# Two pieces of deferred work in a chunked scan: sums of squares in the next scan's first step, the sample's state in its second

## The chip, the core and the metric

The kernel runs on one core of a Trainium2 chip. The metric is device time in microseconds (us) of one execution, as the median of several runs. The core has engines that each run their own instructions in order and meet through semaphores: TensorE (PE in the profile, PEld for its weight loads), VectorE (DVE), ScalarE (ACT), GpSimd (POOL) and SyncE (SP), which issues most DMAs.

## What is computed

A trunk of two layers for 1024 prompt tokens and 64 sample tokens (8 sequences of 8), 1024 channels wide, in float32. The first layer is a Mamba-2 mixer, the second a pooling mixer. The change lies in the first layer, in the scan over the sequence and the gated norm behind it. Cut to that:

```python
def ssd_branch(h, conv_prev, ssm_prev, ...):
    zxbcdt = h @ w_in                                  # z, x, B, C, dt
    xbc_act = silu(conv(xbc))
    ...
    y, new_ssm = ssd_scan(xs, dt, A, Bm, Cm, ssm_prev) # 32 heads in 8 groups, chunks of 128 tokens
    y = y + d_skip * xs
    gated = (y * silu(z)).reshape(b, L, 8, 256)        # 8 groups of 256 channels
    gated = gated * rsqrt(mean(gated * gated, -1) + EPS)
    return (gated * norm_g) @ w_out, new_conv, new_ssm

def ssd_scan(x, dt, A, B, C, h0):
    ...
    chunk_states = einsum('bctgn,bctgr,bctgrp->bcgrpn', B, decay_end, xdt)
    h = chunk_decay * h + chunk_states                 # from chunk to chunk
    y_inter = einsum('bctgn,bctgr,bcgrpn->bctgrp', C, exp(acum), h_prev)
    return y_intra + y_inter, h_final
```

The sample's sequences have one chunk of 8 tokens each, start from a given state h0, and give back a new state (`new_ssm`), which is an output.

## The kernel before

Channels lie on the 128 partitions, tokens along the free dimension (1024 prompt tokens and 64 sample tokens, 1088 columns). After a first stage the eight channel groups g = 0 to 7 are scanned one after the other (`ssd_layer`, `scan`). A scan has four steps p = 0 to 3, each for two chunks of 128 prompt tokens. A step has transposes and products of the next chunks (`scan_front`, PSUM tiles `tr`), the chunk states (`scan_state`, PSUM tile `S`, states `h`), the decay matrices of the next step (`scan_decay`: a DMA broadcasts the cumulated log decays into the single buffer `acb`, ACT makes `ea`, `M` and `cd` from it, DVE multiplies) and the output (`scan_y`, PSUM tiles `y`, added into `xs` by L587). Step 2 also holds the front of the 64 sample tokens (`sample_front`, `sample_inter` with tile `Z`), step 3 their output (`sample_y`).

Between these, TensorE works off units of a fill stream (`fills`): the input projection of the next groups, three units of 24 matmuls for each tile of 128 channels (PSUM tiles `mm`, evicted by ACT in L433 and L435, then convolved). The last tile, (7, 3), is done in eight units over all three `mm` buffers at once. After it the stream goes over to the output projection: rows of gated outputs come back from DRAM (`row<-gyd`, L1583), ACT and DVE split them into two parts (`b<-row`, L1088 and L1089), and products `op<-b,w` follow. `PACE` says how many units each step takes.

TensorE's order is the order in which the code is written; on the other engines and in SP's DMA queue a scheduler orders the instructions, by when it thinks that they can run. Tiles of one row of tokens come from a ring of slots (`Slots`): a slot goes to the tile that asks next, and who had it before decides what that tile waits for.

Four pieces of a scan's end are deferred into the next scan:

- `gate_rows(s)`, at the end of step 3: DVE multiplies the outputs by the gate (L710), ACT squares them (L711).
- `gate_norm(last)`: 16 matmuls with ones sum the squares over channels (PSUM tile `ms`, of the two `y` buffers), ACT takes Ln and Exp (L722, L723), a DMA writes the result out (`rsd`) and another reads it back to all partitions (`rs<-rsd`).
- `gate_scale(last)`: DVE multiplies by it (L732, twice), two DMAs store the rows (`gyd<-xbc`, L734).
- `sample_state(last)`: 16 matmuls give the sample's new state (PSUM tiles `S`: both `y` buffers, the `S` buffer and one `mm` buffer), DVE adds it (L696, four times), two DMAs store it (`hsT`, L697). `sample_load(s)` behind it loads the next sample state (`h<-h0T`) and `acs`.

Of the kernel before, what the change touches and what calls it, by code (L numbers as in the profile page):

```python
# [106 lines left out]
class Build:  # L107
# [1411 lines left out]
    def scan(self, s, fill):  # L1519

        g = s.g
        last, after = self.scans[g - 1] if g else None, self.scans[g + 1] if g < 7 else None
        for p in range(4):
            a, b, c = PACE[g][p]
            self.units(fill, a)
            if p < 3:
                self.scan_front(s, p + 1)
            self.scan_state(s, p)
            if p < 3:
                self.scan_decay(s, p + 1)  # L1530
                if p < 2:
                    self.scan_ac(s, p + 2)
                elif after:
                    self.scan_ac(after, 0)
            self.units(fill, b)
            if p == 3 and g < 6:
                self.silu_burst(after.T)
            self.scan_y(s, p, self.sample_y if p == 3 else None)
            if p == 2:
                self.sample_front(s)  # L1540
                self.sample_inter(s)
            if last and p == int(g < 7):
                self.gate_norm(last)
            self.amtag = "mm" if p in (0, 3) else "y"
            ada = self.ada(g, p)
            next(ada, None)
            if p == 2:
                self.gate_load(s)
                if g == 6:
                    self.silu_burst(after.T[:3])  # L1550
            elif p == 3:
                if g < 7:
                    self.sample_decay(s)
                else:
                    self.gate_rows(s)
            self.units(fill, min(c, 1))
            for _ in ada:
                pass
            if p == int(g == 7):
                if last:  # L1560
                    self.sample_state(last)
                if g < 7:
                    self.sample_load(s)
            if last and p == (2 if g < 7 else 1):
                self.gate_scale(last)
                if g == 7:
                    self.sample_load(s)
            if p == 3 and after:
                if g == 6:
                    self.units(fill, c - 1)  # L1570
                    self.silu_burst(after.T[3:])
                self.scan_front(after, 0)
                self.scan_decay(after, 0)
                self.scan_ac(after, 1)
                self.gate_rows(s)
                if g < 6:
                    self.units(fill, c - 1)
            else:
                self.units(fill, c - min(c, 1))
# [314 lines left out]
```

## Time and profile before

| what | value |
|---|---|
| time, median of 3 runs | 1621.42 us (1621.29 to 1623.38) |
| time of the profiled execution | 1624.89 us |
| its span in the trace | 1622.8 us |
| TensorE busy | 1581.0 us, 97% of the span |
| VectorE, ScalarE, GpSimd busy | 1245.1, 807.6, 460.3 us (77%, 50%, 28%) |
| granted TensorE clock, mean | 0.985 of full speed |

A share is an average over the whole program. The scans take the time from about 280 to 850 us of the span. What a change in one step is worth is read from the waits in that step.

### The profile page before, as it was taken

The page shows a single profiled execution, that of the slowest core. Times are in us where ns is not written, and L with a number is a line of the kernel's source. Part 1 is how long each engine was busy: PE and PEld are TensorE (multiplying, and loading weights), DVE is VectorE, ACT ScalarE, POOL GpSimd, SP SyncE. Part 2 cuts the span into 40 slices and gives each one's busy share as a digit, 9 for nine tenths or more (in the row PEclk, how much of TensorE's full clock was granted, in tenths as well). Part 3 has the DMA queues.
Part 4 walks back from the last instruction along what each step waited for, and adds up shares of the span by engine and source line. Part 5 has one row for each costly group of instructions (what it writes and reads, how often), then busy time and mean ns, then how long its engine had stood idle before and what let it go on. Part 6 is the DMA issues. An engine that isn't in the chain of part 4 may idle for free.

```text
span 1622.8 us, 31026 instructions
## 1 busy us (share of the span) xinstructions
PE 1581.0 (97%) x12399; PEld 1521.3 (94%) x12399; DVE 1245.1 (77%) x1986; ACT 807.6 (50%) x1427; POOL 460.3 (28%) x500
## 2 busy tenths in 40 slices
PE   8999999999999999999799999999999999999997
PEld 6899999999999999998789989999999999999997
DVE  6875476777777777777889878888889777667876
ACT  6653335566657666666654357532323233233363
POOL 0233351212121121213101121665666630000331
PEclk9999999999999999999899999999999999999999
DMA  9422226435454463658599882132333379566673
GB/s 348 164 97 79 98 82 226 138 125 205 149 182 145 155 213 118 211 146 273 141 344 296 211 195 85 71 122 106 113 113 104 105 250 360 145 173 177 159 163 113
DMA packets 103782, 271.74 MB, mean 167 GB/s; under 512 B 17724, under 2 KB 41688, under 8 KB 103640
## 3 DMA queue, kind: packets, MB, share of 16 engines
q1 hardware_dynamic: 95576, 244.35, 43.4%
q0 software_dynamic: 8064, 25.43, 8.9%
q8 instruction: 97, 1.59, 0.4%
q14 instruction: 45, 0.37, 0.1%
HBM read 208.43 MB, written 56.86 MB: 163 GB/s over the span
## 4 chain that ended last, share of the span: by engine, by line
PE 87%; issue 4%; DVE 4%; ACT 2%; DMA 2%; POOL 1%; SPq 0%; DVEq 0%; POOLq 0%; ACTq 0%
PE st L98 29%; PE mm L98 28%; PE op L98 14%; PE y L98 3%; PE pl L98 3%; PE S L98 2%; PE am L98 2%; PE tr L101 1%; PE tr L98 1%; PE ms L98 1%; DMA x<-xT 1%; PE p L98 1%; DMA wr<-wout 0%; DVE rst L1315 0%; PE Z L98 0%
## 5 line engine op out<-in xcount | busy, mean ns | idle before, releaser
L98 PE MATMUL op<-b,w 128*128 128x272 f32 x2688 | 349.6, 291 | 10.9 <-ACT w L1148 5.3
L98 PEld LDWEIGHTS op<-b,w 128*128 128x128 f32 x2688 | 343.3, 191 | 16.2 <-ACT w L1148 6.0
L98 PE MATMUL st<-hh,w 128*128 128x272 f32 x1408 | 273.8, 289 | 0.0
L98 PE MATMUL mm<-hh,wh 128*128 128x364 f32 x720 | 246.8, 343 | 0.0
L98 PE MATMUL mm<-hl,wh 128*128 128x364 f32 x720 | 236.9, 329 | 0.0
L98 PE MATMUL mm<-hh,wl 128*128 128x364 f32 x720 | 236.7, 329 | 0.0
L98 PEld LDWEIGHTS st<-hh,w 128*128 128x128 f32 x1408 | 224.6, 188 | 0.3 <-issue 0.3
L98 PE MATMUL st<-t,w 128*128 128x272 f32 x1584 | 205.3, 287 | 0.0
L98 PE MATMUL st<-hl,w 128*128 128x272 f32 x704 | 203.4, 289 | 0.0
L98 PEld LDWEIGHTS st<-t,w 128*128 128x128 f32 x1584 | 201.0, 188 | 0.0
L98 PEld LDWEIGHTS mm<-hh,wh 128*128 128x128 f32 x720 | 135.8, 189 | 14.0 <-issue 9.7
L187 ACT ACTIVATE w<-wr 128x512 fp32r<-128x512 f32 x88 | 55.5, 631 | 176.3 <-PE st L98 143.0
L98 PEld LDWEIGHTS mm<-hl,wh 128*128 128x128 f32 x720 | 135.9, 189 | 0.7
L98 PEld LDWEIGHTS mm<-hh,wl 128*128 128x128 f32 x720 | 135.8, 189 | 0.0
L98 PEld LDWEIGHTS st<-hl,w 128*128 128x128 f32 x704 | 132.6, 188 | 0.0
L579 POOL TENSOR_TENSOR hd<-h,cd 128x256 f32<-128x256 f32 x56 | 70.7, 1262 | 116.1 <-ACT cd L560 58.4
L1168 DVE SCALAR_TENSOR_TENSOR x<-op,gat,x 128x272 f32<-128x272 f32 (+1 forms) x160 | 72.7, 478 | 34.5 <-PE op L98 31.4
L358 DVE SCALAR_TENSOR_TENSOR raw<-raw,vec,raw 128x1112 f32<-128x1112 f32 x64 | 90.3, 1411 | 10.0 <-ACT raw L356 9.7
L363 POOL COPY ncv<-raw 128x3 f32<-128x3 f32 x32 | 17.1, 533 | 277.9 <-ACT raw L433 267.0
L1148 ACT ACTIVATE w<-wr 128x1024 fp32r<-128x1024 f32 x56 | 59.0, 1054 | 69.1 <-PE op L98 55.0
L946 DVE TENSOR_TENSOR u<-st,u 128x272 f32<-128x272 f32 (+1 forms) x158 | 61.4, 409 | 40.1 <-PE st L98 38.1
L189 POOL TENSOR_TENSOR w<-wr,w 128x512 fp32r<-128x512 f32 x44 | 79.5, 1806 | 37.9 <-ACT w L187 37.6
(272 smaller groups left out, 3216.9 us busy)
## 6 DMA issues: line engine op xcount, KB each, us to landing
wr<-win SPq DMA_DIRECT2D x48, 512.0 KB, 4.0
acb<-acd SPq DMA_DIRECT2D x32, 512.0 KB, 3.8
wr<-pin SPq DMA_DIRECT2D x32, 512.0 KB, 3.5
wr<-wout SPq DMA_DIRECT2D x28, 512.0 KB, 6.5
wr<-pout SPq DMA_DIRECT2D x28, 512.0 KB, 4.6
row<-gyd SPq DMA_DIRECT2D x22, 544.0 KB, 6.7
wr<-wout POOLq DMA_DIRECT2D x20, 512.0 KB, 8.3
wr<-pout POOLq DMA_DIRECT2D x20, 512.0 KB, 5.9
```

What stands on the lines that cost most here:

```text
L98: return self.pin(self.build.nc.tensor.matmul(*a, **k))
L101: return self.pin(self.build.nc.tensor.transpose(*a, **k))
L187: self.nc.scalar.activation(hi, src, AF.Copy)
L189: eng.tensor_tensor(out=lo, in0=src, in1=hi.bitcast(F32), op=ALU.subtract)
L358: nc.vector.scalar_tensor_tensor(out=acc[:, :n], in0=raw[:, k:k + n], scalar=w[k], in1=acc[:, :n], op0=ALU.mult, op1=ALU.add)
L363: nc.gpsimd.tensor_copy(ncv[:, 0:1, :], raw[:, 1024:1027].unsqueeze(1))
L579: nc.gpsimd.tensor_tensor(out=hd, in0=h, in1=cd[:, :, cc].unsqueeze(2).to_broadcast([P, 4, 64]), op=ALU.mult)
L946: nc.vector.tensor_tensor(out=out, in0=x, in1=y, op=ALU.add)
L1148: self.nc.scalar.activation(hi, r, AF.Copy)
L1168: ins = nc.vector.scalar_tensor_tensor(out=x[e][:, a:a + pn], in0=ps[:, :pn], scalar=g, in1=x[e][:, a:a + pn], op0=ALU.mult, op1=ALU.add)
```

## The change

`gate_norm` of the scan before moves from step 1 to step 0; `sample_state` of the scan before moves from step 0 to step 1, and `sample_load` with it. This holds for scans g = 1 to 6: at g = 0 there is no scan before and `sample_load` stays in step 0, and at g = 7 the two conditions give the steps that they gave already. `gate_scale` is called in step 2 as before. No operation is added or removed.

```diff
             if p == 2:
                 self.sample_front(s)
                 self.sample_inter(s)
-            if last and p == int(g < 7):
+            if last and p == 0:
                 self.gate_norm(last)
             self.amtag = "mm" if p in (0, 3) else "y"
             ada = self.ada(g, p)
...
             self.units(fill, min(c, 1))
             for _ in ada:
                 pass
-            if p == int(g == 7):
+            if p == int(g > 0):
                 if last:
                     self.sample_state(last)
                 if g < 7:
```

The scheduler orders the other engines anew around this. Three places of scan 6 are shown, where the numbers behind a name are only a count of tiles.

VectorE, from the end of step 1 of scan 6 to the front of the sample in step 2 (`xd` is read from the `tr` tiles of step 2's transposes; `rs` is scan 5's norm), before:

```order
L587 SCALAR_TENSOR_TENSOR xbc_7485<-xbc_7485,vec,y_8205 128x256
L561 TENSOR_TENSOR M_8154<-M_8154,cb_8150 128x1024
L587 SCALAR_TENSOR_TENSOR xbc_7706<-xbc_7706,vec,y_8205 128x256
L562 TENSOR_TENSOR ea_8328<-xbc_7307,ea_8328 128x1024
L732 SCALAR_TENSOR_TENSOR xbc_6696<-xbc_6696,vec,rs_8236 128x1088
L732 SCALAR_TENSOR_TENSOR xbc_6917<-xbc_6917,vec,rs_8236 128x1088
L545 TENSOR_TENSOR xd_8310<-tr_8300,tkx 128x2x256
L580 TENSOR_TENSOR h_8315<-hd_8316,S_8312 128x256
L358 SCALAR_TENSOR_TENSOR raw_8292<-raw_8176,vec,raw_8292 128x1112
L580 TENSOR_TENSOR h_8319<-hd_8320,S_8312 128x256
L358 SCALAR_TENSOR_TENSOR raw_8292<-raw_8176,vec,raw_8292 128x1112
L545 TENSOR_TENSOR xd_8310<-tr_8300,tkx 128x2x256
```

and with the change:

```order
L587 SCALAR_TENSOR_TENSOR xbc_7485<-xbc_7485,vec,y_8193 128x256
L587 SCALAR_TENSOR_TENSOR xbc_7706<-xbc_7706,vec,y_8193 128x256
L732 SCALAR_TENSOR_TENSOR xbc_6696<-xbc_6696,vec,rs_8033 128x1088
L732 SCALAR_TENSOR_TENSOR xbc_6917<-xbc_6917,vec,rs_8033 128x1088
L561 TENSOR_TENSOR M_8142<-M_8142,cb_8138 128x1024
L696 TENSOR_TENSOR h_126_7450<-h_126_7450,S_8238 128x512
L696 TENSOR_TENSOR h_127_7452<-h_127_7452,S_8239 128x512
L696 TENSOR_TENSOR h_126_7450<-h_126_7450,S_8240 128x512
L696 TENSOR_TENSOR h_127_7452<-h_127_7452,S_8241 128x512
L562 TENSOR_TENSOR ea_8328<-xbc_7295,ea_8328 128x1024
L545 TENSOR_TENSOR xd_8310<-tr_8300,tkx 128x2x256 x2
L1149 TENSOR_TENSOR w_8594<-wr_8474,w_8593 128x1024
```

The two L732 now stand ahead of the decay products, the four L696 behind them, and both L545 right behind L562, followed by a weight split (L1149) that stood ahead of the later L1089 before.

ScalarE at the same place (`mm_8264` is the last projection unit before tile (7, 3); `row_8362` is row 0), before:

```order
L722 ACTIVATE z_7642<-ms_8224,eps 128x272
L557 ACTIVATE M_8330<-acb_8168,tka_1658 128x128
L723 ACTIVATE z_7642<-z_7642 128x272
L552 ACTIVATE ea_8328<-acb_8168 128x1024
L557 ACTIVATE M_8330<-acb_8168,tka_1658 128x128 x2
L558 ACTIVATE M_8330<-M_8330 128x1024
L560 ACTIVATE cd_8340<-acb_8168 128x8
L433 ACTIVATE raw_8176<-mm_8238 128x364
L1148 ACTIVATE w_8593<-wr_8474 128x1024
L433 ACTIVATE raw_8176<-mm_8264 128x296
L435 ACTIVATE raw_8176<-mm_8264 128x8x8
```

and with the change:

```order
L433 ACTIVATE raw_8164<-mm_8167 128x364
L557 ACTIVATE M_8142<-acb_7965,tka_1657 128x128 x4
L557 ACTIVATE M_8142<-acb_7965,tka_1658 128x128 x4
L558 ACTIVATE M_8142<-M_8142 128x1024
L560 ACTIVATE cd_8152<-acb_7965 128x8
L433 ACTIVATE raw_8164<-mm_8212 128x364
L552 ACTIVATE ea_8328<-acb_8156 128x1024
L557 ACTIVATE M_8330<-acb_8156,tka_1657 128x128 x4
L557 ACTIVATE M_8330<-acb_8156,tka_1658 128x128 x4
L558 ACTIVATE M_8330<-M_8330 128x1024
L433 ACTIVATE raw_8164<-mm_8264 128x296
L435 ACTIVATE raw_8164<-mm_8264 128x8x8
```

The decay exponentials of the step before (M_8142, from the `acb` before) now stand behind the convolution instead of ahead of it, and the eviction of `mm_8264` stands behind the next decay's L552, L557 and L558, which need `acb_8156`.

SP's queue at the same place, before:

```order
L697 DMA hsT<-h_124_7272 128x1024
L697 DMA hsT<-h_125_7274 128x1024
L519 DMA acb_8168<-acd 128x4x256
L1119 DMA wr_8597<-wout 128x1024
L1583 DMA row_8362<-gyd_73 128x1088
L724 DMA rsd_126<-z_7642 4x272
L727 DMA rs_8236<-rsd_126 128x1088
L519 DMA acb_8344<-acd 128x4x256
L1583 DMA row_8373<-gyd_74 128x1088
L734 DMA gyd_83<-xbc_6696 128x1088
L734 DMA gyd_84<-xbc_6917 128x1088
```

and with the change:

```order
L727 DMA rs_8033<-rsd_126 128x1088
L1119 DMA wr_8597<-wout 128x1024
L734 DMA gyd_83<-xbc_6696 128x1088
L519 DMA acb_8156<-acd 128x4x256
L734 DMA gyd_84<-xbc_6917 128x1088
L1583 DMA row_8521<-gyd_80 128x1088
L697 DMA hsT<-h_126_7450 128x1024
L697 DMA hsT<-h_127_7452 128x1024
L1583 DMA row_8362<-gyd_73 128x1088
L519 DMA acb_8344<-acd 128x4x256
L1583 DMA row_8373<-gyd_74 128x1088
```

The last `acb` of the scan (acb_8168, now acb_8156) went from a place behind the state's stores to one behind the row store gyd_83, and rows 0 and 1 (row_8362, row_8373) to places behind the stores of the state, whose two slots they now take over. Row 7 (row_8521) takes the slot that gyd_83 is stored from.

## Rows read from the trace of the kernel before

**Rows 1.** First line of the profile page.

```profile
span 1622.8 us, 31026 instructions
```

**Rows 2.** Stretches: length; busy us of PE, PEld, DVE, ACT, POOL; clock; DMA share, GB/s.

```profile
340.00:740.00 400.00, 400.00 (x3316) 372.98 (x3313) 311.57 (x433) 257.88 (x524) 85.70 (x140) 1.00 0.51 168
755.10:761.20 6.10, 6.10 (x40) 4.71 (x41) 6.10 (x11) 4.29 (x7) 0.00 (x0) 0.50 0.98 397
785.10:798.80 13.70, 7.45 (x29) 6.58 (x30) 12.27 (x22) 10.11 (x15) 0.86 (x1) 0.50 0.74 189
```

**Rows 3.** Waits of TensorE over the scans (290 to 870 us).

```profile
PE tr L98 <- DVE xd L545: 3.2, 1, 3.2
```

**Rows 4.** Timeline of TensorE, scans 6 and 7: start, duration, instructions, [idle before <- releaser].

```profile
721.16 1.15 PE L98 MATMUL S<-Ms,Bs 32*128 32x256 f32 x16
...
734.33 1.12 PE L98 MATMUL ms<-z,ones 128*32 128x272 f32 x16
...
746.41 0.33 PE L98 MATMUL mm<-hh,wh 128*128 128x360 f32 x1
...
755.10 1.55 PE L98 MATMUL tr<-kc,xbc 128*64 128x128 f32 x12 [3.15 <-DVE xd L545]
...
770.66 1.01 PE L98 MATMUL op<-b,w 128*128 128x272 f32 x6
...
785.91 1.33 PE L101 MATMUL tr<-kc,xbc 128*128 128x128 f32 x5 [2.89 <-ACT xbc L394]
```

**Rows 5.** Timeline of VectorE, same columns, scan 6.

```profile
722.33 2.48 DVE L696 TENSOR_TENSOR h<-h,S 128x512 f32<-128x512 f32 x4 [0.69 <-PE S L98]
...
737.33 0.47 DVE L587 SCALAR_TENSOR_TENSOR xbc<-xbc,vec,y 128x256 f32<-128x256 f32 x1
...
747.30 2.62 DVE L732 SCALAR_TENSOR_TENSOR xbc<-xbc,vec,rs 128x1088 f32<-128x1088 f32 x2 [5.88 <-DMA rs<-rsd]
...
750.44 0.41 DVE L580 TENSOR_TENSOR h<-hd,S 128x256 f32<-128x256 f32 x1
...
754.27 0.68 DVE L545 TENSOR_TENSOR xd<-tr,tkx 128x512 f32<-128x512 f32 x1
...
763.45 1.22 DVE L1149 TENSOR_TENSOR w<-wr,w 128x1024 fp32r<-128x1024 f32 x1
764.79 3.90 DVE L1089 TENSOR_TENSOR b<-row,b 128x544 fp32r<-128x544 f32 x6
```

**Rows 6.** Timeline of ScalarE, same columns, scans 6 and 7.

```profile
705.71 2.11 ACT L711 ACTIVATE z<-xbc 128x1088 f32<-128x1088 f32 x2
...
724.41 1.06 ACT L552 ACTIVATE ea<-acb 128x1024 f32<-128x1024 f32 x1 [3.01 <-DMA acb<-acd]
...
728.81 0.20 ACT L560 ACTIVATE cd<-acb 128x8 f32<-128x8 f32 x1
...
736.65 1.58 ACT L557 ACTIVATE M<-acb,tka 128x128 f32<-128x128 f32 x5 [3.67 <-DMA acb<-acd]
...
756.90 0.66 ACT L1088 ACTIVATE b<-row 128x544 fp32r<-128x544 f32 x1 [3.75 <-PE tr L98]
...
781.43 1.06 ACT L1135 ACTIVATE wr<-wr 128x1024 f32<-128x1024 f32 x1 [8.32 <-DMA wr<-wout]
```

**Rows 7.** Timeline of SP's queue: when it issued these DMAs.

```profile
719.34 0.38 SPq L519 DMA_DIRECT2D acb<-acd  x1
...
729.03 0.38 SPq L519 DMA_DIRECT2D acb<-acd  x1
...
771.96 1.25 SPq L616 DMA_DIRECT2D acs<-acd  x1
```

**Rows 8.** DMA issues of the whole span: count, KB each, median us from issue to landing.

```profile
acb<-acd SPq DMA_DIRECT2D x32, 512.0 KB, 3.8
row<-gyd SPq DMA_DIRECT2D x22, 544.0 KB, 6.7
```

**Rows 9.** All 16 stores of the sample's state, hsT: us to landing.

```profile
DMA to landing us min/median/max: 2.6/3.1/9.3
```

## The prediction

> **What bounds the kernel now.** The profiled execution took 1624.89 us, 2.1 of them outside its span [rows 1]; it lies 3.5 us above the median of 1621.42, so I sum in its trace and take the difference off the median. The view by stretches comes first: from 340 to 740 us, which holds scans 1 to 5 and the first half of scan 6, TensorE is busy for 400.00 of 400.00 us at full clock [rows 2]. In those scans the change can win nothing; it can only lose, by a wait that is not there now. So the second view is TensorE's own waits over the scans, and the one to see is the 3.2 us for DVE's `xd` [rows 3]. The timeline puts it at 755.10, at the sample's transposes in step 2 of scan 6 [rows 4]. DVE's timeline says why: `gate_scale` (L732) of scan 5 stands ahead of `xd` (L545) and waited 5.88 us for the norm's DMA; the second L545 came only at 754.27, ended at 754.95, and TensorE went on [rows 5]. Behind that gap TensorE ran 6.10 us at clock 0.50, 1.2 GHz instead of 2.4, and was busy throughout [rows 2]; the same work at the upper level takes 3.05 us. So 3.15 + 3.05 = 6.2 us hang on this one stall.
>
> **The change, scans 1 to 5.** Sixteen `ms` matmuls (1.12 us) and sixteen `S` matmuls (1.15 us) trade places [rows 4]; the work is the same. Two waits could appear. First, `ms` needs the squares. The last L711 of scan 5 ends at 705.71 + 2.11 = 707.8 [rows 6]. `ms` would start where the outputs of step 0 end; the `S` of that step starts at 721.16 [rows 4], and one unit and the modulation matmuls, about 5.5 us, lie between, so some 715.6: 7.8 us to spare, and the other scans have the same pattern. Second, `S` in step 1 needs a `y` buffer back, which two L587 release. `S` would start one unit (4.1 us by the pitch of the same matmuls) behind 734.33, at 738.4 [rows 4]; even at the old pace two L587 in a row from 737.33 end at 738.2 [rows 5]. I count both at nothing; uncovered, either would cost its lateness times five. The later `h<-h0T` load and state store have most of a step as cover.
>
> **Scan 6: what the stall becomes.** Today it takes 747.30 - 734.33 = 13.0 us from `ms` to L732 [rows 4, 5]. With `ms` at 715.6 the norm is there at about 729, and DVE comes to L732 behind the two L587. These start between 734.33, when TensorE ends the outputs, and 737.33, the old pace [rows 4, 5]. I take 735.3, near the lower end: DVE loses the 2.48 us of L696 in step 0 [rows 5], and ACT's convolution no longer queues behind 728.81 + 0.20 - 725.47 = 3.5 us of exponentials [rows 6]. The first L732 then ends at 735.3 + 0.9 + 1.3 = 737.5. So the 5.88 us are gone.
>
> What is late next is the last `acb` of the scan. SP has it behind gyd_83, which waits for that L732: issued at 737.8 (739.8 at the old pace). Its landing is 3.8 us in the median [rows 8]; of the two in this scan one took 724.41 - 719.34 = 5.1, the other, among stores and weight loads, 736.65 - 729.03 = 7.6 [rows 6, 7]. The state's stores are behind it now, so I take 4.5, between the first two: it lands at 742.3. ACT needs 728.81 - 724.41 = 4.4 us from a landing to the end of its exponentials [rows 6]; only then it evicts mm_8264, with 0.6 us: 747.3. Tile (7, 3) wants that buffer for its third chunk, now at 746.41 [rows 4]. **A new wait of 0.9 us**, queued behind which is all of TensorE's fill. `xd` is done by then (L562 and both L545 by about 746), so the sample's transposes wait for nothing and the clock has no long gap to fall in.
>
> Behind that DVE decides, not TensorE. L1149 (1.22 us) now stands ahead of L580 and waits for ACT's weight split, by estimate 1.2 us behind the eviction of 747.3: L580 at 749.8 instead of 750.44, 0.6 us sooner. From there to the state that the outputs of step 3 need, DVE has one L545 (0.68) and one L1149 (1.22) less [rows 5]. TensorE would be 5 us ahead, but waits there: products `op` start 0.6 + 0.7 + 1.2 = 2.5 us sooner than 770.66 [rows 4]. Next is the 2.89 us wait at 785.91 for a silu [rows 4], which ACT does behind a sign change (L1135) that waits 8.32 us for a weight load [rows 6]. SP issued that load behind `acs`, which held it 1.25 us [rows 7]; the change puts it ahead. So it comes 2.5 + 1.1 = **3.6 us sooner**, and the silu with it. What follows to 800 us is DVE's work in line (12.27 busy of 13.70 us [rows 2]) and moves as a whole; so do the output projection and the pooling layer, whose DMAs are released by compute. Sum: 1624.9 - 3.6 = 1621.3 in the profiled time; off the median, 1617.8.
>
> **A rule weighed.** A store of the state took 2.6 to 9.3 us to land, 3.1 in the median [rows 9]. The Trainium skill, "DMA: Bandwidth & Descriptors", section "Anatomy of one DMA — SWDGE (gpsimd) path", gives a DMA a nearly constant 2.0 us and the bytes at 436 GB/s, for a path other than SP's. An estimate from that page is 3.2 us for 512 KB, which agrees with the median and not with 9.3; by the page the third rival below would drop out and 1617.8 would stand, by the rows it keeps its chance.
>
> **Rivals.**
> *The new wait eats the gain (no change).* If `acb` takes 7.6 us, it lands at 745.4, mm_8264 is free at 750.4, and TensorE waits 4.0 us, longer than the 3.15 removed, with the low clock behind it as before. L580 comes at 750.4 + 1.2 + 1.2 = 752.8, 2.4 us late, less 1.9 of DVE work, less 1.1 for `acs`: 0.6 us gained, 1620.8. For it: the row store just ahead in the queue; against: the heavy traffic of 729 came with the state's stores, which are gone from there.
>
> *The low clock of 785 goes as well (faster).* With the 2.89 us wait shorter, the clock may stay up from 785.10 to 798.80. TensorE was busy 7.45 us of it at 0.50 [rows 2], half of which is 3.7; about 1 us of that lies ahead of a wait for DVE. 3.6 + 2.7 = 6.3, 1615.1. Against: DVE stays the slower one there, so gaps remain.
>
> *Row 0 comes late (slower).* Rows 0 and 1 take the slots of the stored state, so SP holds row 0 until the store has landed. With L696 done at 742.3 and 3.1 us [rows 9] it is issued at 745.4 and lands 6.7 later [rows 8], at 752.1, before ACT goes on (it waits for step 2's outputs, 755.10 - 3.15 + 0.9 = 752.9). If the store takes 9.3 us [rows 9], and row 7, ahead in the queue, holds it to 743.9, row 0 lands at 759.9; ACT's next row split, now at 756.90 [rows 6], follows some 2 us of ACT work later, at 761.9, and all behind it is 5.0 late, less 1.1: 3.9 slower, 1625.3. It decides from a landing at 756.0 on (no gain) and is more than 3.2 us from 759.2 on. The skill's same page, "Rules for kernel authors", asks for a DMA to be issued early and waited for late; this half of the change does the opposite.
>
> **How the numbers follow.** 0.2% is 3.2 us, about what runs of this kernel can tell from no change. My forecast gets 0.48, by its bounds (landing 3.8 to 5.1, pace of L587) from 1 to 5.5 us gained, so a bit over half of it beyond 3.2. The eaten gain gets 0.22, the second clock 0.15, the late row 0.15. Faster: 0.28 + 0.15 = 0.43 or a little more; slower: 0.10 of the late row and 0.06 of an `acb` still later; same: the rest. The range runs from 1613.5 (1.6 us below the second clock's case) to 1624.0, which leaves out most of the late row; my forecast's own is 1616 to 1620.5.
>
> **What would show it.** Right: no TensorE wait for `xd` before the sample's transposes in scan 6, clock 1.00 there, L732 without a wait, a wait of about 1 us at the third chunk of tile (7, 3), 400 to 740 us still without a gap. Wrong: a gap of 3 us or more at tile (7, 3); L1088 waiting for row 0; a wait at `ms` or `S` in scans 1 to 5, which would come five times.

## The result and the profile after

The changed kernel takes 1630.35 us in the median (1628.46 to 1631.90), beside 1621.36 for the kernel before: a ratio of 1.0052, 95% interval 1.0035 to 1.0070. It is slower by 8 to 9 us, where 3.6 us of gain were forecast. The profiled execution took 1629.01 us. One execution of a later experiment (`acb_first`: 2547.80 us at a mean granted clock of 0.557, where its others had 0.986 to 0.991) is left out of that experiment's ratio.

The first place to look is the stretch that was full before [rows 2]. In the profile after (span; stretch: length, busy us of PE, PEld, DVE, ACT, POOL, clock, DMA share, GB/s):

```profile
span 1627.1 us, 31034 instructions
```

```profile
340.00:740.00 400.00, 395.45 (x3255) 367.68 (x3252) 303.90 (x426) 252.61 (x510) 78.86 (x138) 1.00 0.50 164
```

TensorE now idles 4.55 us in that stretch. Its waits from 290 to 870 us (engine, line, releaser: us in total, times, longest) name the new one, `mp`, five times, once in each scan:

```profile
PE y L98 <- DVE h L580: 4.3, 2, 3.8
PE am L98 <- ACT mp L266: 4.1, 5, 1.0
...
PE mm L98 <- ACT raw L435: 1.6, 1, 1.6
```

The `xd` wait at the sample's transposes [rows 3] is gone, as predicted. In TensorE's timeline stand one of the five waits, in scan 3, and the three that matter in scans 6 and 7:

```profile
538.68 0.82 PE L98 MATMUL tr<-kc,xbc 128*64 128x128 f32 x12
...
546.25 0.61 PE L98 MATMUL am<-kc,mp 128*128 128x9 f32 x4 [0.59 <-ACT mp L266]
...
753.53 0.43 PE L98 MATMUL mm<-hh,wh 128*128 128x360 f32 x1 [1.60 <-ACT raw L435]
...
774.97 0.69 PE L98 MATMUL y<-ea,h 128*64 128x128 f32 x4 [3.80 <-DVE h L580]
...
796.35 1.51 PE L101 MATMUL tr<-kc,xbc 128*128 128x128 f32 x6 [4.38 <-DVE xd L545]
```

`mp` is ScalarE's copy of the first half of a modulation block (`ada_block`, L266); the second half, `am<-kc,mp`, stands in TensorE's order one unit behind the sample's front. In the kernel before it began 543.79 - 536.97 = 6.8 us behind the sample's transposes and found `mp` ready:

```profile
536.97 0.82 PE L98 MATMUL tr<-kc,xbc 128*64 128x128 f32 x12
...
543.79 0.51 PE L98 MATMUL am<-kc,mp 128*128 128x9 f32 x4
```

ScalarE in scan 3, before and after:

```profile
509.88 2.44 ACT L557 ACTIVATE M<-acb,tka 128x128 f32<-128x128 f32 x8
...
513.32 0.20 ACT L560 ACTIVATE cd<-acb 128x8 f32<-128x8 f32 x1
...
541.11 0.36 ACT L266 ACTIVATE mp<-am 128x256 f32<-128x256 f32 x1
541.37 0.62 ACT L652 ACTIVATE Bs<-tr,kc 128x128 f32<-128x128 f32 x2
```

```profile
521.36 2.46 ACT L557 ACTIVATE M<-acb,tka 128x128 f32<-128x128 f32 x8 [1.22 <-PE y L98]
...
524.81 0.20 ACT L560 ACTIVATE cd<-acb 128x8 f32<-128x8 f32 x1
...
529.95 1.06 ACT L552 ACTIVATE ea<-acb 128x1024 f32<-128x1024 f32 x1 [3.73 <-DMA acb<-acd]
...
545.30 0.62 ACT L652 ACTIVATE Bs<-tr,kc 128x128 f32<-128x128 f32 x2 [2.39 <-DVE Ms L648]
545.82 0.38 ACT L266 ACTIVATE mp<-am 128x256 f32<-128x256 f32 x1
```

Two things differ. The scheduler now puts the copies `Bs` (L652) ahead of `mp`; and `Bs` waits 2.39 us for VectorE's L648, which comes 5.9 us behind the sample's transposes instead of 3.6. VectorE in scan 3, before and after:

```profile
540.56 0.68 DVE L648 TENSOR_TENSOR Ms<-tr,tks 128x512 f32<-128x512 f32 x1
```

```profile
531.04 1.23 DVE L562 TENSOR_TENSOR ea<-xbc,ea 128x1024 f32<-128x1024 f32 x1 [1.76 <-ACT ea L552]
...
544.59 0.68 DVE L648 TENSOR_TENSOR Ms<-tr,tks 128x512 f32<-128x512 f32 x1
```

One cause of its lateness can be read there: it waited 1.76 us for `ea`, which ScalarE began 3.73 us late for want of `acb`. SP's queue, before and after:

```profile
513.54 0.38 SPq L519 DMA_DIRECT2D acb<-acd  x1
```

```profile
524.19 0.33 SPq L734 DMA_DIRECT2D gyd<-xbc  x1
525.03 0.38 SPq L519 DMA_DIRECT2D acb<-acd  x1
525.50 0.52 SPq L734 DMA_DIRECT2D gyd<-xbc  x1
```

With the 1.7 us by which the scan as a whole is behind, `acb` leaves 9.8 us later now. It stands behind a row store there, but that is not what held it: `acb` has a single buffer, and L560 is the last that reads the `acb` before. L560 ended at 524.81 + 0.20 = 525.01, and SP issued at 525.03; before it ended at 513.52, and SP issued at 513.54. In the other scans it left within 0.2 us of the end of L560 as well, but in scan 4 only 1.0 us behind it, with the row store between.

L560 is late because the exponentials ahead of it (L557) now wait for the `y` products of step 1. Their tile `M` shares two buffers with the sample's `Ms` (L553 and L645, tag `M`), and the products of `sample_state` are the last that read `Ms`. Before, these ran at 506.92 in step 0, and L557 ran at 509.88 without a wait; with the change they run at 525.64, so that `Ms` holds its buffer a step longer and `M` needs the one that step 1's `y` products still read. The addresses of these tiles in the built program say the same.

So `mp` was done 541.11 + 0.36 - 536.97 = 4.5 us behind the transposes before, and 545.82 + 0.38 - 538.68 = 7.5 us after, where it is due at about 6.9.

### The profile page after: what moved, and what is told of

Its sections match the earlier page's. It is cut to its first block, busy times and chain, and to the rows that moved or that the text cites. A ratio compares the mean times of both kernels' runs of the same rounds, so it can differ in the third digit from the quotient of the medians.

```text
span 1627.1 us, 31034 instructions
## 1 busy us (share of the span) xinstructions
PE 1581.3 (97%) x12399; PEld 1520.1 (93%) x12399; DVE 1242.3 (76%) x1986; ACT 807.2 (50%) x1427; POOL 460.5 (28%) x500
## 4 chain that ended last, share of the span: by engine, by line
PE 77%; DVE 5%; DMA 5%; ACT 5%; issue 5%; POOL 2%; SPq 0%; DVEq 0%; POOLq 0%; ACTq 0%
PE st L98 29%; PE mm L98 23%; PE op L98 14%; PE y L98 3%; PE pl L98 3%; DMA acb<-acd 2%; PE am L98 2%; PE S L98 1%; ACT M L557 1%; PE tr L101 1%; DMA x<-xT 1%; PE ms L98 1%; PE tr L98 1%; DMA hsT<-h 1%; POOL hd L579 1%
## 5 line engine op out<-in xcount | busy, mean ns | idle before, releaser
L98 PEld LDWEIGHTS op<-b,w 128*128 128x128 f32 x2688 | 344.1, 191 | 18.1 <-ACT w L1148 7.3
L579 POOL TENSOR_TENSOR hd<-h,cd 128x256 f32<-128x256 f32 x56 | 77.9, 1390 | 143.0 <-ACT cd L560 79.9
L1148 ACT ACTIVATE w<-wr 128x1024 fp32r<-128x1024 f32 x56 | 59.1, 1055 | 68.3 <-PE op L98 55.2
L557 ACT ACTIVATE M<-acb,tka 128x128 f32<-128x128 f32 x256 | 78.9, 389 | 17.4 <-PE y L98 17.4
```

The source lines that it names most:

```text
L98: return self.pin(self.build.nc.tensor.matmul(*a, **k))
L557: nc.scalar.activation(M[:, r, t], acb[:, r, t], AF.Relu, bias=self.tka[cc][:, col + r:col + r + 1], scale=-1.0)
L579: nc.gpsimd.tensor_tensor(out=hd, in0=h, in1=cd[:, :, cc].unsqueeze(2).to_broadcast([P, 4, 64]), op=ALU.mult)
L1148: self.nc.scalar.activation(hi, r, AF.Copy)
```

## The experiments

Two theories for scans 1 to 5 were tested: **late acb** (the last `acb` of a scan queues behind `gyd`, so ScalarE and VectorE come late) and **order** (`Bs` ahead of `mp` on ScalarE does it by itself). The buffer `M` was in neither; what the same traces show of it stands with each run. For scan 6: the predicted gain is there and is eaten by named waits, or it was never there. Ratios are to the kernel before in the same series. The last two columns are of the profiled execution: TensorE's waits from 290 to 890 us added up, and the time from the sample's inter-chunk products of scan 5 (`Z`) to the `op` products that wait 1.07 us for L1148, which is the passage through scans 6 and 7.

| kernel | ratio (95%) | waits, us | passage, us |
|---|---|---|---|
| before, three executions | 1 | 17.1, 16.6, 15.8 | 193.1, 191.4, 186.7 |
| whole change, again | 1.0059 (1.0041 to 1.0078) | 23.6 | 193.1 |
| change in scans 1 to 5 only | 1.0053 (1.0036 to 1.0071) | 22.2 | 191.7 |
| change in scan 6 only | 1.0020 (1.0007 to 1.0034) | 18.5 | 190.8 |
| sums of squares only | 1.0042 (1.0029 to 1.0055) | 18.5 | 192.9 |
| sample's state only | 1.0040 (1.0025 to 1.0055) | 17.2 | 190.8 |
| sums of squares in scan 6 only | 1.0025 (1.0015 to 1.0036) | 18.8 | 195.9 |
| change, `acb` first | 1.0029 (1.0018 to 1.0041) | 14.5 | 189.4 |
| change, `mp` first | 1.0026 (1.0012 to 1.0039) | 18.1 | 190.5 |
| change, both first | 1.0007 (0.9995 to 1.0019) | 15.7 | 190.6 |
| change in scan 6 only, `acb` first | 0.9998 (0.9985 to 1.0010) | 16.3 | 189.3 |

### The halves of the change

Sums of squares only (`norm_only`), from the kernel before:

```diff
-            if last and p == int(g < 7):
+            if last and p == 0:
                 self.gate_norm(last)
```

> Only the sums of squares move to step 0; the sample's final state stays in step 0. In SP's queue the last acb of a scan then stands ahead of the gyd stores again, while on ACT the two copies Bs (L652) stand ahead of mp (L266) in step 2, as in the changed kernel. Late-acb theory (TensorE's five waits for mp come from the acb that queues behind gyd): no wait for mp over 0.3 us in scans 1 to 5, stretch 340 to 740 us busy for 400 us, and of scan 6's gain what the prediction named, so 1617 to 1621 us. Order theory (the waits come from Bs ahead of mp on ACT alone): the five waits of 0.6 to 1.0 us stay, 1622 to 1626 us.

1625.52 us, 1.0042, in the range of the order theory, but not for its reason: there is no wait for `mp`, although `Bs` stands ahead of it. The order alone is not enough. But there was another loss in scans 1 to 5 that neither theory had. ScalarE's and TensorE's waits (290 to 755 and 290 to 890 us):

```profile
ACT wh L152 <- DMA wr<-win: 21.7, 4, 5.9
```

```profile
PE y L98 <- DVE h L580: 9.7, 4, 4.7
```

The weight load (`wr<-win`) stands in SP's order behind the two `gyd` stores and an `h<-h0T` that waits for them to land, and the state `h` comes late behind ScalarE's and VectorE's split of that weight. But it needed its own buffer too: in scan 3 VectorE's split of the weight before, now behind the decay products, ended at 525.91 + 1.21 = 527.12, and SP issued the load at 527.20, against 515.75 before. `acb` was on time here (L560 ended at 516.49, SP issued at 516.52): with the state in step 0, `Ms` is free again.

Sample's state only (`state_only`):

```diff
-            if p == int(g == 7):
+            if p == int(g > 0):
                 if last:
                     self.sample_state(last)
```

> Only the sample's final state (and the next sample's load) moves to step 1; the sums of squares stay in step 1. The last acb is ahead of gyd in SP's queue, Bs ahead of mp on ACT. Late-acb theory: no wait for mp in scans 1 to 5; the row scale's wait for rs in scan 6 stays, so TensorE's 3 us wait for xd and the low clock behind it stay: 1620 to 1623 us. Order theory: the waits for mp stay, 1624 to 1628 us.

1626.20 us, 1.0040, over the range of late acb and within that of order. One wait for `mp` was left, 1.5 us. `acb` left at 522.60 in scan 3, right behind an L560 that ended at 522.57, and here no `gyd` stood ahead of it: the move of the state makes `acb` late by itself. Its waits are only 0.1 to 1.4 us more than those of the kernel before. From the sample's `Z` products in scan 1 to those in scan 5 it took 288.2 us, 3.0 to 3.3 us more than the kernel before (284.8 to 285.1); the rest of its 6.5 us stays open.

### By scans

Scans 1 to 5 only (`scans_1_5`), then scan 6 only (`scan_6`), both from the changed kernel:

```diff
-            if last and p == 0:
+            if last and p == int(g == 6):
...
-            if p == int(g > 0):
+            if p == int(0 < g < 6 or g == 7):
```

> The change in scans 1 to 5 only, scan 6 as before. If the loss is made in scans 1 to 5 (waits for mp): five such waits, 395 to 396 us of work in the stretch 340 to 740 us, and 4 to 6 us slower than before. If it is made in scan 6 and later, where the predicted gain should have been: within 2 us of before.

```diff
-            if last and p == 0:
+            if last and p == int(g < 6):
...
-            if p == int(g > 0):
+            if p == int(g > 5):
```

> The change in scan 6 only, scans 1 to 5 as before. By the prediction's step for scan 6: 3.6 us faster than the profiled execution of before, and no wait of TensorE before 740 us. If the low clock that this step counted as a gain belongs to that execution and not to the kernel, the gain over the median of before is nothing or it is a loss: 1 to 5 us slower, from the waits behind the late acb and before the y products (1.6 and 3.8 us in the changed kernel).

1629.45 us, 1.0053: the loss is made in scans 1 to 5. All five waits are there, 4.1 us, and TensorE is busy for 395.90 of the 400 us. Scan 6 alone took 1622.95 us, 1.0020: a loss of 1 to 5 us, not a gain of 3.6. TensorE waited there for the eviction and the `y` products:

```profile
749.36 0.44 PE L98 MATMUL mm<-hh,wh 128*128 128x360 f32 x1 [1.48 <-ACT raw L435]
...
773.21 0.69 PE L98 MATMUL y<-ea,h 128*64 128x128 f32 x4 [5.50 <-DVE h L580]
```

Ahead of the second one ScalarE stood twice for rows (`b<-row`), which SP had issued behind the state's stores:

```profile
744.40 1.06 ACT L552 ACTIVATE ea<-acb 128x1024 f32<-128x1024 f32 x1 [4.25 <-DMA acb<-acd]
...
755.12 0.66 ACT L1088 ACTIVATE b<-row 128x544 fp32r<-128x544 f32 x1 [3.29 <-DMA row<-gyd]
...
761.04 0.66 ACT L1088 ACTIVATE b<-row 128x544 fp32r<-128x544 f32 x1 [4.00 <-DMA row<-gyd]
```

```profile
738.12 0.33 SPq L734 DMA_DIRECT2D gyd<-xbc  x1
738.97 0.38 SPq L519 DMA_DIRECT2D acb<-acd  x1
...
742.65 0.94 SPq L697 DMA_DIRECT2D hsT<-h  x2
750.93 0.33 SPq L1583 DMA_DIRECT2D row<-gyd  x1
```

Row 0 left only at 750.93, 8.3 us behind the first store. That is the prediction's third rival.

Sums of squares in scan 6 only (`scan6_norm`), from the kernel before:

```diff
-            if last and p == int(g < 7):
+            if last and p == int(g < 6):
```

> Only the sums of squares move, and only in scan 6; the sample's state and all of scans 1 to 5 stay as before. If the removed stall of 3 us at the sample's transposes is worth what the prediction said: no wait for xd there, 1616 to 1619 us beside a before of 1620 us. If a wait of like size takes its place at the y products in scan 7 (DVE's L580 behind late rows or a late weight load): 1620 to 1623 us.

1625.27 us beside 1622.06, 1.0025: slower, about as much as the second case allowed at most. The `xd` wait went, and two waits for `h` took its place, one of them already in scan 6; why `h` was late there was not followed:

```profile
738.75 0.69 PE L98 MATMUL y<-ea,h 128*64 128x128 f32 x4 [4.00 <-DVE h L580]
774.99 0.69 PE L98 MATMUL y<-ea,h 128*64 128x128 f32 x4 [4.60 <-DVE h L580]
```

### The repairs

`acb` kept ahead of `gyd` in SP's queue, with TensorE's order untouched (`acb_first`; the row store is wrapped in the same way):

```diff
-        self.nc.sync.dma_start(s.acb[p], self.acd[...])
+        (self.tc.keep_in_program_order if p == 3 else id)(self.nc.sync.dma_start(s.acb[p], self.acd[...]))
```

> The changed kernel, with the last acb of each scan kept ahead of the two gyd stores in SP's queue; TensorE's order is the same. Late-acb theory: ACT's 4 us waits for acb, the five waits of TensorE for mp (4.1 us together) and the 1.6 us wait for the eviction in scan 6 go; about 5 to 6 us back, 1623 to 1625 us. Order theory: the waits for mp stay; only the eviction's 1.6 us can go, 1627 to 1630 us.

1624.52 us, 1.0029: late acb's time. No wait for `mp` is left, with `Bs` still ahead of it. But the theory had the wrong reason. ScalarE and SP's queue in scan 3:

```profile
523.03 0.19 ACT L560 ACTIVATE cd<-acb 128x8 f32<-128x8 f32 x1
...
527.12 1.06 ACT L552 ACTIVATE ea<-acb 128x1024 f32<-128x1024 f32 x1 [2.69 <-DMA acb<-acd]
...
543.02 0.63 ACT L652 ACTIVATE Bs<-tr,kc 128x128 f32<-128x128 f32 x2 [1.86 <-DVE Ms L648]
543.54 0.38 ACT L266 ACTIVATE mp<-am 128x256 f32<-128x256 f32 x1
```

```profile
523.25 0.38 SPq L519 DMA_DIRECT2D acb<-acd  x1
```

`acb` left no sooner: 13.7 us ahead of the sample's transposes (536.93), as in the changed kernel, and again right behind L560. What changed is its way: with the row stores behind it ScalarE went on 3.9 us after the issue, not 4.9 (3.9 against some 5 in scans 2 and 4 too). So ScalarE waited for it for 2.69 us instead of 3.73, VectorE's L648 came 5.4 us behind the transposes, 0.5 us sooner than in the changed kernel but far from 3.6, and `mp` was done 7.0 us behind them, just when TensorE wanted it. From `Z` in scan 1 to `Z` in scan 5 this kernel took 286.5 us, still 1.4 to 1.7 us more than the kernel before. In scan 6 the eviction's wait did not go; it was 2.3 us.

`mp` ahead of `Bs` on ScalarE, by writing the two copies behind it (`mp_first`):

```diff
-        for i in range(2):
-            nc.scalar.activation(Bt[:, i], pt[:, 256:384], ...)
+        s.late = lambda: [
+            nc.scalar.activation(Bt[:, i], pt[:, 256:384], ...) for i in range(2)]
...
             next(ada, None)
             if p == 2:
-                self.gate_load(s)
+                s.late(), self.gate_load(s)
```

> The changed kernel, with the two copies Bs written behind the copy mp, so that mp is ahead on ACT in step 2 of scans 1 to 5; acb is as late as in the changed kernel. Order theory: the five waits for mp go, 4 us back, 1624.5 to 1627 us. Late-acb theory in its strict form (ACT is so late that any place in its queue is too late): the waits shrink by less than half, 1628 to 1630 us.

1623.59 us, 1.0026. The waits are gone and the stretch from 340 to 740 us is full:

```profile
340.00:740.00 400.00, 400.00 (x3313) 373.41 (x3309) 308.58 (x433) 256.13 (x518) 84.16 (x140) 1.00 0.51 167
```

```profile
541.00 0.36 ACT L266 ACTIVATE mp<-am 128x256 f32<-128x256 f32 x1
543.66 0.62 ACT L652 ACTIVATE Bs<-tr,kc 128x128 f32<-128x128 f32 x2 [2.30 <-DVE cb L654]
```

`mp` is done 4.5 us behind the transposes (536.85) again, though `acb` is as late as in the changed kernel. From `Z` to `Z` the scans take 285.1 us, as before. So the waits need both: `Bs` ahead of `mp`, which ties `mp` to VectorE, and VectorE late in that step. Either repair takes them away, the one with 2.4 us to spare, the other with nothing. Late acb as the whole cause and order by itself have both fallen, and so has the place behind `gyd` as the reason why `acb` leaves late. A third buffer for `M`, or `sample_state` on a tile of its own, was not tried.

Both repairs (`both_first`):

> The whole change, with acb ahead of gyd in SP's queue and with mp ahead of Bs on ACT. If both conditions are needed for the waits for mp, taking away the second one as well adds nothing: no such wait, 400 us of work between 340 and 740 us, and the time of the two single repairs, 1622 to 1625 us. If what is left of their loss (4 us over before) is lateness of acb or order on ACT, it is faster than either, 1618 to 1621 us.

1622.37 us beside 1622.06 (the kernel before was 0.7 to 2.1 us slower in this series than in the others), 1.0007: no difference from the kernel before that can be measured. The interval just overlaps those of the single repairs, so that the second one adds something is likely but not settled. If it does, it is not in scans 1 to 5: from `Z` to `Z` these take 285.1 us here too.

The change in scan 6 only, with `acb` ahead of `gyd` there (`scan6_acb_first`): the wrapped lines of `acb_first`, with `p == 3 and s.g == 6` and `s.g == 5` as conditions.

> The change in scan 6 only, with the last acb of that scan kept ahead of the gyd stores in SP's queue; scans 1 to 5 as before. If the late acb and the row loads that stand with it eat scan 6's gain: no wait of TensorE for the y products at 770 to 775 us (5.5 us with the change in scan 6 alone), and 1 to 3 us faster than with the change in scan 6 alone, 1618 to 1621 us beside a before of 1620 us. If scan 6's passage is set by something else (DVE's work in line up to 870 us): the same as with the change in scan 6 alone, 1622 to 1624 us.

1621.22 us, 0.9998. The wait for the `y` products is gone, and the loss of scan 6 with it; a gain does not come. The eviction's wait is still there, and the output products now wait for rows:

```profile
747.88 0.67 PE L98 MATMUL mm<-hh,wh 128*128 128x360 f32 x1 [2.33 <-ACT raw L435]
...
770.68 0.93 PE L98 MATMUL op<-b,w 128*128 128x272 f32 x3 [0.39 <-DVE b L1089]
772.99 9.52 PE L98 MATMUL op<-b,w 128*128 128x272 f32 x74 [1.39 <-DVE b L1089]
```

This edit also moves the stores of the rows behind row loads. The traces tell the two apart in part: `acb` again left right behind L560 (736.63) and ScalarE went on 5.2 us later, against 5.4 with the change in scan 6 alone, so `acb` came hardly sooner. SP issued the first three rows from 746.92 on, where with the change in scan 6 alone row 0 left at 750.93, and ScalarE no longer waited for rows ahead of the `y` products.

### The same kernels again

The changed kernel once more (`after_again`):

> The changed kernel, unchanged, on this chip beside the partial changes. Late-acb theory and order theory alike: 1628 to 1632 us, five waits for mp of 0.6 to 1.0 us again, 4 to 5 us lost between 340 and 740 us. If the waits for mp were an accident of one execution, they are not there and the time is under 1626 us.

1628.86 us, 1.0059, with the five waits again (4.0 us) and 394.85 us of work in the stretch. The loss is no accident of one execution.

The kernel before, twice more (`before_again`, `before_third`):

> The kernel before, unchanged, for a second profiled execution. If the profiled execution that the prediction was made from is an unusual one (its mean granted clock was 0.985, other executions of it 0.989 to 0.991), this one shows less than 13.7 us of low clock at 785 us, or none at 755 us, and a span of 1615 to 1619 us. If low clock at those two places belongs to every execution, it shows both again and a span of 1621 to 1623 us.

> The kernel before, for a third profiled execution; the first had a span of 1622.8 us, the second 1619.5 us, and its unprofiled executions have a median of some 1618 us. If the first two were unlucky in the clock: a span of 1615 to 1618 us with less low clock between 750 and 830 us, and the same waits of TensorE. If executions differ by their waits: other waits at 755, 785, 793 and 821 us (3.2, 2.9, 5.4 and 3.6 us in the first).

Their spans were 1619.5 and 1616.5 us, against 1622.8 in the one that the prediction was made from [rows 1]. The stall on which it rested [rows 4] in the second and the third execution, each with the clock around it:

```profile
753.80 1.44 PE L98 MATMUL tr<-kc,xbc 128*64 128x128 f32 x12 [2.68 <-DVE xd L545]
```

```profile
745.00:765.00 20.00, 17.32 (x136) 15.50 (x135) 18.46 (x26) 12.25 (x22) 6.34 (x4) 0.91 0.94 339
```

```profile
752.20 0.88 PE L98 MATMUL tr<-kc,xbc 128*64 128x128 f32 x12 [1.23 <-DVE xd L545]
```

```profile
745.00:765.00 20.00, 18.17 (x174) 16.45 (x172) 19.49 (x29) 14.01 (x26) 9.71 (x4) 1.00 0.92 349
```

3.15, 2.68 and 1.23 us, and in the fastest execution the clock stayed at 1.00 behind it. The 2.89 us wait at 785 us was 1.83 and 0.96 us there. What differed lies ahead of VectorE's L732 (747.30, 746.00 and 744.41 us in the three): ScalarE's exponentials in front of the norm's Ln and Exp began at 736.65, 734.74 and 734.07, and from the issue of `rsd` to L732 it took 8.1, 8.7 and 7.8 us. The third execution also has a wait for `h` at the `y` products, 1.6 us. Executions differ by their waits, and by the low clock behind them.

## Why the prediction was wrong

**Scans 1 to 5 at nothing: this step failed.** Of the two waits that it asked about, neither came. It asked only what `ms` and `S` themselves need, and for the moved state only how much cover its load and store have. It did not ask whose buffer the moved products hold: `Ms` stays in one of the two `M` buffers a step longer, ScalarE's exponentials wait for step 1's `y` products, and `acb` leaves 8.7 to 9.8 us later in scan 3 in every kernel that moves the state there, 0.9 us in the one that moves the sums of squares alone. With `Bs` ahead of `mp` this costs TensorE 4.0 to 4.1 us in five waits. Taking the waits away in either of two ways brings the ratio from 1.0052 to 1.0026 (`mp` first) and 1.0029 (`acb` first); with both it is 1.0007.

The waits understate the loss: from `Z` in scan 1 to `Z` in scan 5 the changed kernel took 290.2 and 291.0 us, 289.6 with the change in scans 1 to 5 only, and 285.1 with `mp` first, against 284.8 to 285.1 before. So 4 to 6 us are lost there, with four of the five waits, which idle for 3.4 us in the changed kernel. A wait costs more than its idle time: in scan 3, where TensorE idled 0.59 us, the first `mm` behind `am` began 546.72 - 545.34 = 1.38 us behind the last one ahead of it, against 544.16 - 543.63 = 0.53 before, so 0.85 us more. What the 1.0053 of scans 1 to 5 alone has beyond that is not settled.

**Scan 6, the stall.** It went, and the clock over the sample's front stayed up (1.00 from 745 to 765 us), as predicted. The size was wrong: 3.15 + 3.05 = 6.2 us was what hung on it in one execution. In another it was 1.23 us with no low clock behind it, so other executions had less to win.

**Scan 6, the late `acb`.** The time was right by luck, the reason was not. Where the five waits are repaired and scan 6 starts on time (`mp` first), SP issued `acb` at 737.38, for which 737.8 had been forecast. But the step let `acb` wait for L732 and gyd_83. SP issued gyd_83 at 736.53; `acb` left when L560 of the step before had ended, at 737.36. Those are the exponentials that the prediction saw move behind the convolution, and it took only the gain from that. With `acb` ahead of `gyd` it still left right behind L560 (736.63 in `scan6_acb_first`). ScalarE had it at 742.94 (742.3); the landing took 5.6 us, not 4.5. The new wait was 1.60 us there, 1.60 and 1.48 in the whole change and in scan 6 alone, and 4.28 in the repeated change, not 0.9.

**Behind it.** The step gave the `op` products 2.5 us sooner, behind a wait of TensorE. The wait at the `y` products was 3.80 us in the changed kernel, 1.29 when repeated (where the eviction's wait had been 4.28), 5.50 with the change in scan 6 alone and 6.09 with `mp` first. With the eviction's wait that is 5.4 to 7.7 us, in place of the stall and the silu wait, which were 6.0, 4.5 and 2.2 us together in the three executions of the kernel before (the third waited 1.6 us at the `y` products too). The rival "row 0 comes late", at 0.15, is what scan 6 did in three of these four: SP issued row 0 some 8 us behind the state's stores, and ScalarE waited for it and for the row behind it. What remains is nothing to a few us lost: the passage through scans 6 and 7 took 190.5 to 193.1 us with the whole change, 186.7 to 193.1 without.

**The rule weighed.** The Trainium skill, "DMA: Bandwidth & Descriptors", section "Anatomy of one DMA — SWDGE (gpsimd) path", has a nearly constant cost, told for a path other than SP's; the estimate of 3.2 us from it would have ruled this rival out. Here the state's stores took 3.9 to 7.4 us in the changed kernel (4.0 in the median), and the measurement decides. The same page of the Trainium skill, "Rules for kernel authors", has a DMA issued early and waited for late. The traces agree: the state's move made `acb` leave 9.8 us later and ScalarE wait 3.73 us for it, and the norm's move made `wr<-win` leave later (527.20 against 515.75).

## What to carry to other kernels

When a scheduler orders the engines, moving a piece of work can move DMAs and copies that stood around it, and it moves the moment at which the tiles that it reads come free. List those tiles, see who takes their buffers next, and read the order of each engine and queue at each repetition of the loop; ask of each instruction that slipped who needs it and by when, also where the engine is full now. An instruction behind another one in a queue need not have waited for it: compare its start with the end of everything that it needs. A loss of 1 us that repeats five times outweighs a stall of 3 us that happens once. And before a stall of one execution is counted as a gain, look at how much executions of the kernel differ; here it was two fifths of the size in another one.

## What the runs showed of the hardware

In one series on one chip, 23 executions of the kernel before took 1613.84 to 1626.21 us. Row loads (`row<-gyd`, 544 KB, from 735 to 770 us) landed after 5.6 to 5.8 us in the fastest profiled execution of the kernel before, 3.4 to 6.1 us in the first one, and 4.1 to 11.5 us with the change in scan 6 only: loads of one size differed by three times. No run isolates why, but one pair of runs bears on it: `acb` (512 KB), issued between two row stores, reached ScalarE after 4.9 to 5.1 us in scans 2 to 4 of the changed kernel, and after 3.9 us where the row stores came later (`acb_first`).
